# A hybrid layer's recurrences: the end of one block and the start of the next written step by step in turn

## The chip, the cores and the metric

The kernel runs on one core of a Trainium2 chip. The core has a matrix engine (TensorE, PE in the profile), a vector engine (VectorE, DVE), a scalar engine (ScalarE, ACT), a general engine (GpSimd, POOL) and a queue that issues transfers (SyncE, SP). Each works through its own queue in order and waits on semaphores for the others. The metric is the device time of one launch in microseconds; lower is better.

## The reference, cut to what matters

The input is one sequence of 2048 tokens with 1024 features; 16 learned tokens are put in front (T = 2064 tokens). One layer is computed in 32-bit floats:

```
p = rms_norm(h) @ w_in                     # 1024 -> 512 (LRU) + 1544 (attention) + 1024 (RWKV)
oa = rg_lru(...)                           # causal conv, gates, h_t = a_t h_{t-1} + b_t, times gelu
ob = forgetting_attention(q, k, v, f)      # 8 heads of 64, causal softmax with a decay term
oc = rwkv7(...)                            # 4 heads of 64, below
h = h + rms_norm(concat(oa, ob, oc) @ w_out)
f = causal_dwconv3(rms_norm(h) @ ffn_up)   # 1024 -> 2 x 2816
h = h + rms_norm((gelu(gate) * val) @ ffn_down)
```

The RWKV group is a recurrence over the tokens, with a state S of 64 x 64 for each head:

```
s_kk = S @ kk_t
S = S * w_t - outer(s_kk, kk_t * a_t) + outer(v_t, k_t)
o_t = S @ r_t
```

The decay w_t, the gate a_t and the vectors come from the projected features by small projections; after the recurrence follow a norm for each head, a bonus term and an output gate.

## The kernel before

**Stages.** First comes the input projection, in three parts of the sequence; beside it run the two recurrences (RWKV and RG-LRU). Then comes attention in two halves of the queries, with the output projection filled in; then the feed-forward part. Every large product is made of three matmuls on split operands (lines 174 to 176: high by high, low by high, high by low).

**The input projection.** In each part it goes through tiles of columns; one *unit* is one tile of 128 columns with one block of tokens, 24 matmuls into the tile `psp`. It writes its result to a scratch array in DRAM, `scr["p"]`, from which recurrence and attention load.

**The recurrence.** `Rwkv.block(b)` works on one block of 256 tokens (block 8: 64), in chunks of 64 tokens. It is a generator: each `yield` ends a step. It has two sections.
- The *opening* makes everything that doesn't need the state: mixing with the token before, the small projections (tile `eps`, lines 1049 to 1100), the products inside a chunk (L1124, tile `rps`), their transposes (L1153) and a triangular solve of 15 dependent turns, a product on POOL (L1171) and a sum on DVE (L1172) each. It ends with `yield self.SOLVED`.
- The *ending* has ten steps: the solve's small blocks are combined by 32 x 32 products (L1195 on PE, with DVE's L1205, L1212, L1219 and copies L1226, L1231 between them), then 64-wide products (L1247 and L1262, copied from PSUM by DVE's L1248 and L1263 and ACT's L1249 and L1264), L1274, the four turns of the state (L1282 on PE, L1286 on DVE), the outputs (L1313, L1318), the norm (L1323 to L1331), the gate (L1338, L1342) and the store (L1352) into `scr["mix"]`.

`lru_block` does the RG-LRU for the same tokens, in four steps (gates L1433, L1434; scan L1451; store L1461).

All PSUM tiles of the recurrence come from two pools: `rps` has two buffers, `eps` has one.

**How they are put beside each other.** `recurrences(..., part)` is a generator over the steps for three blocks. It is driven by `Beside` (PACE = 1.25 steps for each unit of the projection, from the fourteenth of part 0 on). What is left at the end of the projection is run by `beside.finish()`, and the very last ending, that of block 8, by the loop behind it; then the recurrence's memory is given back by `rec.close()`.

**What sets the order.** The program is written in that order, and a scheduler then builds each engine's queue: it takes the written order as a priority and lets instructions of other work pass where its plan has something late. So a change in the written order changes all queues, also beyond the lines that are edited.

**Attention's first tiles.** `Attn` takes the keys and queries from DRAM (k L527, q L553 and L554 on SP), and POOL clears and fills rows of the key tiles (L491, L492). Products: row maxima `mx` (L566), scores `sc` (L693, L694), outputs `po` (L716). The first two key tiles take room that the projection gives back after its last `psp`; the third, which the second half of attention begins with, takes room that `rec.close()` gives back.

Of the kernel before, what the change touches and what calls it, by code (L numbers as in the profile page):

```python
# [445 lines left out]
class Attn:  # L446
# [47 lines left out]
    def next(self, s):  # L494
        self.turn[s] = (self.turn[s] + 1) % len(self.ring[s])
        return self.ring[s][self.turn[s]]
# [908 lines left out]
def lru_block(core, R, scr, k, b):  # L1405

    nc = core.nc
    t0 = max(0, Rwkv.start(b))
    n = min(T, Rwkv.start(b + 1)) - t0
    c0 = PAD + t0  # L1410
    tt = nc.vector.tensor_tensor
    stt = nc.vector.scalar_tensor_tensor

    def tl(s):
        return R.t([P, 256], s, bufs=2 if s == "lu" else 1)[:, :n]

    def raw(row, a):
        t = R.t([P, 260], "lraw", bufs=2)[:, : c0 + n - a]
        nc.sync.dma_start(t, scr["p"][row : row + P, a : c0 + n])
        return t  # L1420

    for p in range(2):
        pc = slice(p, p + 1)
        x = raw(P * p, c0 - 3)
        u, r, g, al = (tl("l" + s) for s in ("u", "r", "g", "a"))
        nc.scalar.activation(u, x[:, 3:], AF.Identity, scale=k["conv_w"][:, 6 + p : 7 + p], bias=k["conv_b"][:, pc])
        for i in range(3):
            stt(u, x[:, i : n + i], k["conv_w"][:, 2 * i + p : 2 * i + p + 1], u, op0=ALU.mult, op1=ALU.add)


        ps = R.pe()
        pa, px = ps[:, :n], ps[:, 256 : 256 + n]
        nc.tensor.matmul(pa, k["ga_w"][:, p], u, start=True, stop=True)  # L1433
        nc.tensor.matmul(px, k["gx_w"][:, p], u, start=True, stop=True)  # L1434
        nc.scalar.activation(r, pa, AF.Abs, bias=k["ga_b"][:, pc])
        nc.vector.tensor_scalar(al, pa, k["ga_b"][:, pc], 0.0, op0=ALU.add, op1=ALU.min)
        nc.scalar.activation(g, px, AF.Tanh, scale=0.5, bias=k["rate"][:, 2, pc])
        nc.scalar.activation(r, r, AF.Tanh, scale=0.5)
        nc.scalar.activation(al, al, AF.Exp)
        stt(r, r, 1.0, al, op0=ALU.add, op1=ALU.mult)  # L1440
        stt(g, g, 1.0, u, op0=ALU.add, op1=ALU.mult)
        yield
        nc.scalar.activation(al, r, AF.Exp, scale=k["rate"][:, 0, pc])
        nc.scalar.activation(r, r, AF.Tanh, scale=k["rate"][:, 1, pc])

        tt(u, al, al, op=ALU.mult)
        stt(r, u, 1.0, r, op0=ALU.add, op1=ALU.mult)
        nc.vector.tensor_scalar(r, r, 1e-34, None, op0=ALU.max)
        nc.scalar.activation(r, r, AF.Sqrt)
        stt(g, g, 0.5, r, op0=ALU.mult, op1=ALU.mult)  # L1450
        nc.vector.tensor_tensor_scan(u, al, g, k["h"][:, pc], op0=ALU.mult, op1=ALU.add)  # L1451
        nc.vector.tensor_copy(k["h"][:, pc], u[:, n - 1 : n])

        ya, y = raw(2 * P + P * p, c0), r
        nc.scalar.activation(y, ya, AF.Square)
        nc.vector.tensor_scalar(y, y, 0.044715, 1.0, op0=ALU.mult, op1=ALU.add)
        tt(y, y, ya, op=ALU.mult)
        nc.scalar.activation(y, y, AF.Tanh, scale=0.7978845608028654)
        stt(y, y, 1.0, ya, op0=ALU.add, op1=ALU.mult)
        stt(u, u, 0.5, y, op0=ALU.mult, op1=ALU.mult)  # L1460
        nc.sync.dma_start(scr["mix"][P * p : P * p + P, t0 : t0 + n], u)  # L1461
        yield
# [600 lines left out]
def recurrences(core, R, lk, f_bias, scr, blocks, part):  # L2063


    for blk in blocks:
        gate_block(core, R, f_bias, scr, blk[2])
        yield
    for b in ((0, 1, 2), (3, 4, 5), (6, 7, 8))[part]:
        gen = R.block(b)  # L2070
        while next(gen) != R.SOLVED:
            yield
        yield from R.ending
        R.ending = gen
        yield from lru_block(core, R, scr, lk, b)


_INS = [
# [9 lines left out]
def hybrid_block_kernel(ctx: ExitStack, tc: tile.TileContext, args, out):  # L2088
# [25 lines left out]
    with ExitStack() as p1:  # L2114
# [7 lines left out]
        with ExitStack() as p1a:  # L2122
# [6 lines left out]
            for part in range(3):  # L2129
# [31 lines left out]
                for whole in units:  # L2161
                    if whole and i == READY + 1:
                        beside.add(recurrences(core, R, lk, a["fox_f_bias"], scr, blocks, part))
                    beside.advance()
                    if not whole:
                        continue
                    if part == 1 and i > 1:
                        next(split_out, None)
                    if part and i % 2 == 0:
                        with tc.issue_after(core.loaded.ins):  # L2170
                            next(sums, None)
                    i += 1
# [185 lines left out]
```

## Time and profile before

| | us |
|---|---|
| median of 3 runs | 3013.33 (3009.2 to 3013.38) |
| the profiled execution | 3015.7 |
| its span in the profile | 3014.0, mean clock of PE 0.969 |
| PE, 40 to 875 (projection) | 814.51 busy of 835 |
| PE, 875 to 1123 (first half of attention, rest of the recurrence) | 228.88 busy of 248, clock 0.85 |
| PE, 1123 to 1150 (step to the second half) | 23.97 busy of 27, clock 0.62 |
| PE, 1150 to 1540 | 381.63 busy of 390, clock 1.00 |
| PE, 1540 to 1600 | 47.69 busy of 60, clock 0.86 |
| PE, 1600 to 3014 (feed-forward) | 1388.66 busy of 1414, clock 1.00 |

The stretches are cut by the times at which the last `psp` product (874.96), the first use of the third key tile (1133.16) and the following stages show in the trace. "Busy" is the time in which PE had a matmul in it; the clock is the share of the full TensorE clock that was granted, so busy times clock is work at full speed. In a timeline a row is start, duration, engine, line, operation, written tile <- read tiles, shape, and in square brackets the idle time of the engine before it with what ended it. `x32` means a group of 32 instructions in a row.

### The profile page before, as it was taken

Reading aid. Unit: us, or ns where it says so; the run is one execution under the profiler, and the core shown is the slowest. Engines: PE = TensorE matmul, PEld = TensorE weight load, DVE = VectorE, ACT = ScalarE, POOL = GpSimd, SP = SyncE. Lnnn points to the kernel's source line nnn. Section 1 sums busy time; section 2 is a strip of 40 time slices with the busy share of each in tenths; the row PEclk is TensorE's granted clock in tenths of the full one; section 3 lists DMA queues with packets and bytes.
Section 4 is the critical chain, followed back from the end, with each engine's and each line's share of the span. In section 5 each row is a group of like instructions: output and inputs, shape, how many; then the busy total and the mean of one; then the engine's idle time right before and its main releaser. Section 6 shows DMA issues by size and latency. Waiting matters only on the chain.

```text
span 3014.0 us, 52809 instructions
## 1 busy us (share of the span) xinstructions
PE 2901.1 (96%) x18694; PEld 2488.9 (83%) x18694; DVE 2037.7 (68%) x3937; ACT 1480.0 (49%) x2858; POOL 1324.4 (44%) x1569
## 2 busy tenths in 40 slices
PE   6999999999999999999979999999999999999998
PEld 6998889888886655666558999999999999787887
DVE  5268645665676776556635898798778777656766
ACT  4246333443345554445634666666566665424333
POOL 1001121222223666666852467455645544656443
PEclk8999999999988899999989999999999999999999
DMA  6776569576653347545245565577677764436453
GB/s 216 235 243 209 169 228 319 173 231 202 201 134 82 95 110 214 121 115 121 59 139 165 166 203 179 170 210 217 206 213 217 215 200 129 161 114 220 143 177 119
DMA packets 469190, 530.49 MB, mean 176 GB/s; under 512 B 85710, under 2 KB 355736, under 8 KB 467372
## 3 DMA queue, kind: packets, MB, share of 16 engines
q1 hardware_dynamic: 468156, 526.17, 58.0%
q8 instruction: 147, 2.41, 0.3%
q0 software_dynamic: 768, 0.93, 0.1%
q14 instruction: 119, 0.97, 0.1%
HBM read 368.07 MB, written 158.90 MB: 175 GB/s over the span
## 4 chain that ended last, share of the span: by engine, by line
PE 59%; DVE 5%; POOL 2%; issue 2%; ACT 2%; DMA 1%; SPq 0%; DVEq 0%; POOLq 0%; ACTq 0%
PE psu L174 9%; PE psu L175 9%; PE psu L176 9%; PE po L716 4%; PE psd L174 4%; PE psd L175 4%; PE psd L176 4%; PE mx L566 2%; PE sc L693 2%; PE pswo L174 2%; PE pswo L176 2%; PE pswo L175 2%; PE sc L694 2%; DVE mc L571 1%; ACT p L698 0%
## 5 line engine op out<-in xcount | busy, mean ns | idle before, releaser
L174 PE MATMUL psu<-xo,uw 128*128 128x344 f32 x1848 | 587.9, 322 | 5.9 <-ACT ga L1821 3.3
L175 PE MATMUL psu<-xo,uw 128*128 128x344 f32 x1848 | 592.2, 321 | 0.0
L176 PE MATMUL psu<-xo,uw 128*128 128x344 f32 x1848 | 582.2, 320 | 0.0
L174 PE MATMUL psp<-xh,wh 128*128 128x384 f32 (+2 forms) x1152 | 379.6, 330 | 0.0
L176 PE MATMUL psp<-xh,wl 128*128 128x384 f32 (+2 forms) x1152 | 376.9, 327 | 0.0
L175 PE MATMUL psp<-xl,wh 128*128 128x384 f32 (+2 forms) x1152 | 376.5, 327 | 0.0
L1650 DVE TENSOR_TENSOR uw<-uq,uw 128x512 fp32r<-128x512 f32 x341 | 320.9, 946 | 59.5 <-ACT uw L1649 57.1
L174 PEld LDWEIGHTS psu<-xo,uw 128*128 128x128 f32 x1848 | 346.5, 188 | 7.5 <-ACT ga L1821 3.6
L175 PEld LDWEIGHTS psu<-xo,uw 128*128 128x128 f32 x1848 | 347.8, 188 | 0.0
L176 PEld LDWEIGHTS psu<-xo,uw 128*128 128x128 f32 x1848 | 346.3, 188 | 0.0
L1649 ACT ACTIVATE uw<-uq 128x512 fp32r<-128x512 f32 x462 | 287.7, 627 | 89.7 <-PE psu L176 41.6
L571 DVE TENSOR_REDUCE mc<-mx 128x1 f32<-128x512 f32 (+6 forms) x352 | 190.2, 565 | 117.8 <-PE mx L566 84.3
L698 ACT ACTIVATE p<-sc,bias 128x512 f32<-128x512 f32 (+4 forms) x352 | 197.5, 590 | 142.5 <-PE sc L694 120.5
L1789 DVE SCALAR_TENSOR_TENSOR uy<-psu,ffn_cols,uy 128x342 f32<-128x342 f32 (+1 forms) x390 | 220.5, 567 | 63.5 <-ACT uy L1787 62.5
L1650 POOL TENSOR_TENSOR uw<-uq,uw 128x512 fp32r<-128x512 f32 x121 | 180.6, 1492 | 157.7 <-ACT uw L1649 134.9
L1797 POOL TENSOR_TENSOR uy<-uy,uy 128x342 f32<-128x342 f32 (+1 forms) x132 | 145.8, 1105 | 228.0 <-DVE uy L1789 64.0
L737 POOL TENSOR_TENSOR acc<-acc,p 128x512 f32<-128x512 f32 (+3 forms) x208 | 223.3, 1075 | 45.9 <-DVE acc L737 21.7
L174 PEld LDWEIGHTS psp<-xh,wh 128*128 128x128 f32 x1152 | 219.2, 190 | 8.7 <-issue 7.3
L176 PEld LDWEIGHTS psp<-xh,wl 128*128 128x128 f32 x1152 | 219.1, 190 | 7.0 <-issue 5.1
L175 PEld LDWEIGHTS psp<-xl,wh 128*128 128x128 f32 x1152 | 219.1, 190 | 5.0 <-issue 3.2
L1650 DVE TENSOR_TENSOR fo<-u,fo 128x896 fp32r<-128x896 f32 x88 | 100.9, 1146 | 132.7 <-ACT fo L1649 132.2
L1649 ACT ACTIVATE fo<-u 128x896 fp32r<-128x896 f32 x88 | 81.2, 923 | 208.5 <-PE psd L176 112.6
(483 smaller groups left out, 6426.8 us busy)
## 6 DMA issues: line engine op xcount, KB each, us to landing
uq<-scr_us SPq DMA_DIRECT2D x220, 256.0 KB
uq<-in_ffn_up_dram SPq DMA_DIRECT2D x209, 256.0 KB
wl<-scr_wk SPq DMA_DIRECT2D x48, 512.0 KB
wh<-scr_wk SPq DMA_DIRECT2D x48, 512.0 KB
u<-scr_ff SPq DMA_DIRECT2D x88, 256.0 KB
scr_ff<-uy SPq DMA_DIRECT2D x110, 171.0 KB
raw<-in_w_in_dram SPq DMA_DIRECT2D x24, 512.0 KB
scr_wk<-wh SPq DMA_DIRECT2D x24, 512.0 KB
```

Source lines behind the costliest of these rows:

```text
L174: nc.tensor.matmul(out, ah, bh, start=first, stop=False, skip_group_check=more)
L175: nc.tensor.matmul(out, ah, bl, start=False, stop=False, skip_group_check=more)
L176: nc.tensor.matmul(out, al, bh, start=False, stop=last, skip_group_check=more)
L566: nc.tensor.matmul(ps[:rows, : e - a], q3[:, qo : qo + rows], k2[:, a:e], start=True, stop=not last)
L571: self.reduced = nc.vector.tensor_reduce(mc[:rows, i, ci : ci + 1], ps[:rows, : e - a], axis=AX.X, op=ALU.max)
L698: last = nc.scalar.activation(p[:rows, :w], ps[:rows, :w], AF.Exp, bias=bias[:rows, j : j + 1])
L716: mm = nc.tensor.matmul(po[at : at + 64, c0:n], v1[:rows, j], p[:rows, : n - c0], start=start and i < 2, stop=end and i + 2 >= len(group), ...
L737: eng.tensor_tensor(a, ps_[0][0][:rows, c0:n] if start and i == 1 else a, p[:rows, : n - c0], op=ALU.add)
L1649: core.nc.scalar.activation(hi, src, AF.Copy)
L1650: (eng or core.nc.vector).tensor_tensor(lo, src, hi, op=ALU.subtract)
L1789: core.conved = stt(y[:, :n], src[:, i : n + i], cw[:, 44 * i + cc : 44 * i + cc + 1], y[:, :n], op0=ALU.mult, op1=ALU.add)
L1797: core.pooled = nc.gpsimd.tensor_tensor(v[:, :n], g[:, :n], v[:, :n], op=ALU.mult)
```

## The change

In `recurrences` the steps of a block were written one section after another: the opening of block b, the whole ending of block b-1, the RG-LRU of block b. Now there are two chains: the ending of block b-1, and the opening of block b followed by its RG-LRU. One step of each is written in turn, and when one chain is done, the other goes on alone. The instructions are the same. The opening has one step more (a `yield` after the solve), so a block has 19 steps in place of 18 and the first one 9 in place of 8. The ending of block 8 is left over as before.

```diff
     for b in ((0, 1, 2), (3, 4, 5), (6, 7, 8))[part]:
         gen = R.block(b)
-        while next(gen) != R.SOLVED:
+
+        def opening():
+            while next(gen) != R.SOLVED:
+                yield
             yield
-        yield from R.ending
+            yield from lru_block(core, R, scr, lk, b)
+
+        chains = [R.ending, opening()]
+        while chains:
+            chain = chains.pop(0)
+            for _ in chain:
+                chains.append(chain)
+                yield
+                break
         R.ending = gen
-        yield from lru_block(core, R, scr, lk, b)
```

How the queues of the engines change shows at three places. On PE, inside the projection, the small products of the ending of block 1 (`rps` tiles are PSUM results, `rwxu` and `rwsc` tiles of the recurrence; `psp` is the projection). Before:

```order
L1195 MATMUL rps_3649<-rwxu_3562 32x32 x16
L1195 MATMUL rps_3667<-rwxu_3562 32x32 x32
L176 MATMUL psp_4339<-xh_3093,wl_4308 128x384
L174 MATMUL psp_4339<-xh_3093,wh_4307 128x384
L175 MATMUL psp_4339<-xl_3094,wh_4307 128x384
L176 MATMUL psp_4339<-xh_3093,wl_4308 128x384
L1195 MATMUL rps_3730<-rwxu_3562,rwsc_2159 32x32 x16
```

The changed kernel at the same products, with the projection's rows in the middle left out:

```order
L1195 MATMUL rps_3553<-rwxu_3315 32x32 x16
L1195 MATMUL rps_3571<-rwxu_3315 32x32 x32
L174 MATMUL psp_3876<-xh_3058,wh_3790 128x384
...
L1124 MATMUL rps_3636<-rwrav_3533,rwbk_3540 128x128 x4
...
L1124 MATMUL rps_3649<-rwrav_3533,rwbk_3540 128x128 x4
L1195 MATMUL rps_3698<-rwxu_3315,rwsc_2376 32x32 x16
```

Where four projection matmuls stood ahead of the last group there are now 37 and the next block's chunk products (L1124); in the other endings there are as many or more. Between later groups of the ending (L1247, L1262) there are 17 to 20 in most places. In all, the recurrence's instructions on PE stand in 382 separate pieces beside the projection and attention, before in 374.

On PE, at the end of the projection and the start of attention. Before:

```order
L175 MATMUL psp_10080<-xl_6567,wh_9817 128x256
L176 MATMUL psp_10080<-xh_6566,wl_9818 128x256
L1247 MATMUL rps_9191<-rww_973_7341,rwxf_8880 64x128 x4
L1262 MATMUL rps_9237<-rwsc_7340,rwxu_9169 64x128 x8
L1100 MATMUL eps_9753<-rwsq_9660,bones 128x512
L1262 MATMUL rps_9248<-rwsc_7340,rwxu_9169 64x128 x8
L1274 MATMUL rps_9260<-rww_973_7341,rwsc_7340 64x64 x16
L1282 MATMUL rps_9260<-rstate,rwgt_9235 64x64 x4
```

The changed kernel:

```order
L175 MATMUL psp_10010<-xl_6479,wh_9757 128x256
L1313 MATMUL rps_9530<-rstate,rwrav_7465 64x64 x8
L1318 MATMUL rps_9530<-rww_991_7567,rwsc_7566 64x64 x8
L176 MATMUL psp_10010<-xh_6478,wl_9758 128x256
L1100 MATMUL eps_9866<-rwsq_9733,bones 128x512
L693 MATMUL sc_11235<-q_1458_11146,k_1448_11109 128x512
```

The ending of block 5 now lies ahead of the last projection matmul, where it followed it before; one product of the recurrence (L1100) is left between that matmul and attention.

On PE, the end of the recurrence (L1342 is its last product) and the first use of attention's third key tile (`k_1963`). Before, the end of that stretch:

```order
L1342 MATMUL rps_11081<-rwsg_10414,g_up 128x64
L693 MATMUL sc_13122<-q_1922_12765,k_1453_11120 128x512
L694 MATMUL sc_13122<-q_1452_11118,k_1454_11121 128x512
...
L693 MATMUL sc_13277<-q_1974_12943,k_1448_11109 128x512
L693 MATMUL sc_13282<-q_1974_12943,k_1448_11109 128x512
L566 MATMUL mx_12950<-k_1963_12902,q_1456_11125 128x400
```

The changed kernel:

```order
L1342 MATMUL rps_11081<-rwsg_10421,g_up 128x64
L693 MATMUL sc_12831<-q_1852_12520,k_1453_11120 128x512
L694 MATMUL sc_12831<-q_1457_11129,k_1454_11121 128x512
...
L566 MATMUL mx_12873<-k_1454_11121,q_1451_11114 128x128
L568 LDWEIGHTS identb
L568 MATMUL mx_12873<-futureb,identb 128x128
L766 MATMUL mx_12855<-oh_12852,ones_col 1x512
L566 MATMUL mx_12953<-k_1963_12902,q_1456_11125 128x512
```

The last product of the recurrence moved forward by 53 rows of attention (from its 576th to its 523rd on PE), the first use of the tile by 40 (from the 596th to the 556th). Between the two lay 20 rows, of scores and outputs alone, and now lie 33, with row maxima among them. On SP the recurrence's last store (L1352) is followed by the load of that tile (L527) in both orders.

## The prediction

> **What bounds the kernel now.** I read the page first, for the engine that carries the end; then the stretches of TensorE by stage; then its waits inside the input projection; last the timelines of three places where it loses time. The page:
>
> ```profile
> span 3014.0 us, 52809 instructions
> PE 2901.1 (96%) x18694; PEld 2488.9 (83%) x18694; DVE 2037.7 (68%) x3937; ACT 1480.0 (49%) x2858; POOL 1324.4 (44%) x1569
> PEclk8999999999988899999989999999999999999999
> PE 59%; DVE 5%; POOL 2%; issue 2%; ACT 2%; DMA 1%; SPq 0%; DVEq 0%; POOLq 0%; ACTq 0%
> ```
>
> TensorE (PE) is the bound: 96% busy, and most of the chain that ends last. An edit that removes no matmul can only win idle time of PE, or time in which its granted clock was low. The dips of the clock lie in slices 1, 12 to 14 and 23. By stage, PE alone (columns: stretch, length, busy, clock, DMA share, GB/s):
>
> ```profile
> 45.00:875.00 830.00, 809.51 (x6783) 0.97 0.67 216
> 875.00:1123.00 248.00, 228.88 (x1977) 0.85 0.45 104
> 1123.00:1150.00 27.00, 23.97 (x78) 0.62 0.71 141
> 1150.00:1500.00 350.00, 345.91 (x1603) 1.00 0.49 126
> 1600.00:3014.00 1414.00, 1388.66 (x7794) 1.00 0.59 180
> ```
>
> The input projection runs to 875, the first half of attention with the rest of the recurrence to 1123, the step to the second half to 1150, the rest of attention to 1500. That rest, without the recurrence, is 99% busy at clock 1.00. Whatever the recurrence costs besides its own matmuls therefore lies before 1150, and this change moves only the recurrence. All that follows 1150 I leave as it is: its order on PE is nearly the same, at a cost of nothing as long as it starts in the same state.
>
> **The waits inside the projection.** The ending's small products are the longest wait there (us in total, times, longest), and the second wait of that list is a third of it:
>
> ```profile
> PE rps L1195 <- DVE rwxu L1212: 7.7, 4, 3.5
> PE rps L1195 <- ACT rwsc L1154: 2.5, 2, 1.7
> ```
>
> One of the four, on PE and then on DVE:
>
> ```profile
> 396.70 2.18 PE L1195 MATMUL rps<-rwxu 32*32 32x32 f32 x96
> 398.81 0.44 PE L176 MATMUL psp<-xh,wl 128*128 128x384 f32 x1
> 399.09 0.34 PE L174 MATMUL psp<-xh,wh 128*128 128x384 f32 x1
> 399.27 0.34 PE L175 MATMUL psp<-xl,wh 128*128 128x384 f32 x1
> 399.45 0.34 PE L176 MATMUL psp<-xh,wl 128*128 128x384 f32 x1
> 402.00 1.21 PE L1195 MATMUL rps<-rwxu,rwsc 32*32 32x32 f32 x32 [2.21 <-DVE rwxu L1212]
> 403.63 0.52 PE L175 MATMUL psp<-xl,wh 128*128 128x384 f32 x1
> 403.95 0.52 PE L176 MATMUL psp<-xh,wl 128*128 128x384 f32 x1
> ```
>
> ```profile
> 400.06 0.25 DVE L1172 TENSOR_REDUCE rwix<-rwitmp 128x8 f32<-128x112 f32 x1
> 401.28 0.67 DVE L1212 TENSOR_TENSOR rwxu<-rps,rwxu 32x512 f32<-32x512 f32 x1
> ```
>
> The products end at 398.88 (396.70 + 2.18); VectorE (DVE), whose queue holds steps of the next block's solve and of the LRU ahead of it, finishes the sum that they feed at 401.95: 3.1 us. The queue of PE has four projection matmuls for that time, 0.18 us apart (399.27 to 399.45), so PE stands 2.21 us. Afterwards the matmuls come 0.32 us apart (403.63 to 403.95): the clock is halved. Three stretches of 10 us (busy of PE, PEld, DVE, ACT, POOL; then clock) show that for three of the waits:
>
> ```profile
> 400.00:410.00 10.00, 8.00 (x81) 7.69 (x82) 5.25 (x14) 1.52 (x2) 1.02 (x2) 0.83 0.31 93
> 670.00:680.00 10.00, 10.00 (x109) 8.24 (x107) 8.85 (x21) 4.09 (x8) 3.07 (x5) 0.69 0.31 95
> 760.00:770.00 10.00, 8.38 (x112) 7.91 (x106) 7.24 (x19) 3.64 (x8) 4.12 (x7) 0.66 0.68 213
> ```
>
> Lost to the clock: 1.7 + 3.1 + 3.4 = 8.2 us. With the 7.7 of waiting, these four waits cost 15.9 us, 4.0 each.
>
> In the new order 37 projection matmuls stand between these products and the ones that need the sum, at 0.18 us 6.7 us against the 3.1 needed; for the other blocks it is as many or more. So the four waits should end. What is late next: the DVE steps of the solve, which lay among the early steps of the ending, now lie among its later copies (L1248, L1263). There the order gives 17 to 20 projection matmuls a step, 3.1 to 3.6 us, about the 3.1 that are needed. Ends: all won and nothing new, -16; one wait of 4.0 us in each of the six endings that the projection now carries, 24 - 16 = +8. I take **-8**, half of the win, since spacing and delay are so near.
>
> The Trainium skill ("TensorE: Matmul & The Clock Gate", Part 1) says that the clock gate goes to half after an idle window of about 3.4 us. By it a wait of 2 us costs only itself and this term would be at most -7.7; the rows above show the halving behind a wait of 2.21 us, so I go by them.
>
> **The bursts.** A burst of small products costs the next projection matmul: 0.28 us to its successor (398.81 to 399.09) against 0.18, plus about as much in front. The order cuts the recurrence into 382 pieces on PE in place of 374: 8 x 0.1 to 0.2, **+1**.
>
> **The part boundaries.** At the first boundary:
>
> ```profile
> 280.00:310.00 30.00, 23.68 (x301) 18.47 (x299) 27.66 (x77) 24.00 (x46) 10.69 (x19) 0.67 0.41 138
> ```
>
> DVE is 92% busy and PE has 30 - 23.68 x 0.67 = 14.1 us less than its full work. There the new order has a little less DVE work, at the second boundary more, with three groups of the recurrence in it. I take **+1**, with a third of the 14.1 to either side as ends (-5 and +5).
>
> **The start of attention.** PE, with one group at full clock for comparison; then the queue of SP, POOL, and the stretches:
>
> ```profile
> 327.46 1.20 PE L1274 MATMUL rps<-rww,rwsc 128*64 128x64 f32 x32
> 874.96 0.41 PE L176 MATMUL psp<-xh,wl 128*128 128x256 f32 x1
> 882.81 2.03 PE L1274 MATMUL rps<-rww,rwsc 128*64 128x64 f32 x32
> 887.52 0.46 PE L566 MATMUL mx<-k,q 128*128 128x144 f32 x1
> ```
>
> ```profile
> 880.45 0.45 SPq L553 DMA_DIRECT2D q<-scr_qh  x1
> ```
>
> ```profile
> 883.58 3.60 POOL L492 MEMSET k<- 1x2080 f32 x2
> ```
>
> ```profile
> 880.00:890.00 10.00, 8.84 (x85) 6.48 (x84) 8.36 (x21) 0.00 (x0) 5.71 (x4) 0.50 0.53 119
> 890.00:900.00 10.00, 9.51 (x88) 7.13 (x84) 8.13 (x22) 2.82 (x6) 0.00 (x0) 0.50 1.02 216
> ```
>
> Between the last projection matmul (875.37) and the first of attention (887.52) PE works only for the recurrence: 12.15 us at half clock, worth 7.1 at full (x 1.20 / 2.03), so 5.0 are lost; and 887.5 to 900 at 0.50 loses 6.2: 11.3 in all. The new order puts that work ahead of the last projection matmul, where it costs its 7.1 us, and leaves PE one product before attention. The cover is then gone: attention waits for its own loads and for POOL, which clears and fills two key tiles, two pairs of memsets of 3.60 us each. POOL no longer has a memset of the recurrence in front, so PE should stand about 7.2 us. How long the clock stays halved after that no row tells: not at all gives 7.2 - 11.3 = -4; as long as now, with an empty stretch as long as the present one, 12.15 + 6.2 - 11.3 = +7. I take **-2**: a short empty stretch, and half clock for a few microseconds.
>
> **The step to the second half of attention.** PE, SP, POOL:
>
> ```profile
> 1120.77 0.36 PE L1338 MATMUL rps<-ident,rwxu 64*128 64x64 f32 x1 [3.14 <-DVE rwxu L1331]
> 1122.94 0.69 PE L1342 MATMUL rps<-rwsg,g_up 128*128 128x64 f32 x2
> 1133.16 1.07 PE L566 MATMUL mx<-k,q 128*128 128x400 f32 x3 [0.59 <-POOL k L492]
> ```
>
> ```profile
> 1124.06 0.39 SPq L1352 DMA_DIRECT2D scr_mix<-rwxu  x1
> 1124.54 0.45 SPq L527 DMA_DIRECT2D k<-scr_kh  x1
> ```
>
> ```profile
> 1131.29 1.82 POOL L492 MEMSET k<- 1x2080 f32 x1
> ```
>
> The third key tile takes the recurrence's room. Its chain is: the last products (end 1123.63), the last store, then the load behind it on SP, then POOL's fill, ended at 1133.11, and the first product on the tile: 9.5 us, in which PE has some twenty short matmuls. In 1123 to 1150 PE does 23.97 x 0.62 = 14.9 us of full-clock work, a loss of 12.1; with the wait of 3.14 ahead it is 15.3.
>
> In the new order the recurrence's last product stands 53 rows earlier against attention, and 32 matmuls lie between it and the first use of the tile, scores, row maxima and outputs mixed. At 345.91 / 1603 = 0.216 us each that is 6.9 us against 9.5: 2.6 us of waiting stay, and I allow as much again for the clock. That leaves 5 of 15.3, taken as **-11**. Ends: -15 when nothing remains; 0 when the store still comes as late.
>
> **The sum.** -8 + 1 + 1 - 2 - 11 = -19, from the profiled execution's 3015.7 (span 3014.0): 2996.7. That execution lies 2.4 above the median of 3013.3, so the forecast is **2994**. What a measurement here can tell from no change is 0.2%, 6 us.
>
> **The rivals.**
> *Slower: the waits move to the copies.* Opening and ending now share two PSUM banks and one DVE queue all along. Against a step's 3.1 to 3.6 us stands a delay of 3.1; if the solve's steps hold L1248's or L1263's copies some 0.5 us longer, PE stands at both steps of all six endings, and the row above says that 2 us of standing halve the clock: 12 x 4.0 = 48 against 16 won, +32 where I have -8: **3034**. For it: DVE is the busiest of PE's partners; against: in the old order other steps have passed at that spacing without a wait in the list.
> *Moved evenly.* One such wait an ending, +8 for -8: **3010**, within 0.2%.
> *Attention starts empty.* The empty stretch is as long as the present one and the clock stays halved as now: +7 for -2, **3003**. The gate rule of the Trainium skill's page speaks for this one: an empty stretch of 7 us is two of its windows, and the first matmuls would run at half. The trace has no empty stretch of that length inside the projection to show it.
> *The step does not clear.* The recurrence ends no earlier, since its own chain and not PE's order sets its end: 0 for -11, **3005**. For it: PE's wait of 3.14 for L1331 is a wait for that chain; against: 53 rows of lead.
>
> **How the numbers follow.** The forecast 0.43 (its own range 2982 to 3003), copies 0.21, moved evenly 0.15, empty start 0.12, step not cleared 0.09. Faster by over 0.2% (below 3007): 0.43 + 0.12 + 0.09 less a little where two of them meet, 0.61. Same: 0.15 and that little, 0.17. Slower: 0.22. For 8 in 10 the range takes most of the last case's road, up to 3029, and down to 2976, where about all of the waits and of the step are won.
>
> **What would show it.** Right: no wait of L1195 for L1212 of over 1 us and clocks above 0.9 where now 0.66 to 0.83 stands; the first product of attention at most 8 us behind the last of the projection; the last store of the recurrence at least 8 us earlier against attention, and the 27 us behind it at a clock near 0.9. Wrong: PE waits for DVE's L1248, L1263 or L1286 of several microseconds in sum with half clock behind them; a projection that ends later than its added work (7 to 11 us of recurrence) explains.

## The result and the profile after

The changed kernel takes 3020.0 us (median of 19 runs, 3010.8 to 3027.4), the kernel before, run beside it, 3009.4 (19 runs, 3003.3 to 3017.4). The ratio is 1.0027 (95% interval 1.0019 to 1.0036): 8 us slower by the ratio (the medians lie 10.6 apart), where the forecast was 19 us faster. The time lies inside the range that was given, but on the other side of no change: the range reached that far only to hold the slower rivals. Single executions of either kernel scatter by some 15 us; the profiled one of the changed kernel took 3018.4, and a second trace of each kernel was taken below, so that a stage's difference can be told from scatter.

The page of the changed kernel has the same shape as before, with a little less busy time of PE and a longer span:

```profile
span 3016.7 us, 52807 instructions
PE 2895.9 (96%) x18694; PEld 2494.4 (83%) x18694; DVE 2039.6 (68%) x3937; ACT 1481.6 (49%) x2858; POOL 1308.6 (43%) x1569
PEclk8999899999988899999989999999999999999999
```

To see where the time went, both traces are cut at the same places of the work: the last projection matmul, the first matmul of attention, its 520th and 750th row in PE's queue, the first matmul of the feed-forward part, the end. PE alone (stretch, length, busy, clock, DMA share, GB/s), the kernel before:

```profile
40.00:875.40 835.40, 814.91 (x6812) 0.97 0.67 215
875.40:887.50 12.10, 10.94 (x94) 0.50 0.55 128
887.50:1081.60 194.10, 180.62 (x1608) 0.85 0.42 97
1081.60:1150.20 68.60, 61.08 (x355) 0.83 0.62 135
1150.20:1662.40 512.20, 491.52 (x2249) 0.98 0.48 131
1662.40:3014.00 1351.60, 1326.26 (x7513) 1.00 0.59 182
```

The changed kernel:

```profile
40.00:882.20 842.20, 832.28 (x6982) 0.97 0.66 213
882.20:894.00 11.80, 0.88 (x3) 0.64 0.72 165
894.00:1088.80 194.80, 177.13 (x1608) 0.85 0.41 96
1088.80:1145.70 56.90, 49.09 (x277) 0.94 0.56 129
1145.70:1664.50 518.80, 492.46 (x2247) 0.97 0.48 133
1664.50:3016.90 1352.40, 1327.31 (x7513) 0.99 0.59 182
```

The second traces, at the rows that matter. Of the kernel before (projection, gap, attention's first rows, 750th row to feed-forward):

```profile
40.00:877.50 837.50, 820.73 (x6814) 0.97 0.66 214
877.50:889.60 12.10, 10.94 (x95) 0.50 0.55 128
889.60:1079.50 189.90, 178.47 (x1608) 0.86 0.42 99
1148.10:1661.70 513.60, 491.65 (x2248) 0.98 0.48 131
```

Of the changed kernel:

```profile
40.00:883.80 843.80, 832.01 (x6973) 0.97 0.66 212
883.80:895.30 11.50, 0.80 (x3) 0.61 0.71 170
895.30:1089.80 194.50, 176.13 (x1608) 0.86 0.40 97
1146.50:1665.80 519.30, 492.43 (x2248) 0.97 0.48 132
```

Length less busy time is PE's idle time. Mean of the two traces of each kernel, in us:

| stage | length before | after | idle before | after |
|---|---|---|---|---|
| projection | 836.5 | 843.0 | 18.6 | 10.9 |
| gap ahead of attention | 12.1 | 11.7 | 1.2 | 10.8 |
| attention to its 520th row | 192.0 | 194.7 | 12.5 | 18.0 |
| 520th to 750th row | 68.6 | 56.8 | 7.5 | 7.6 |
| 750th row to the feed-forward part | 512.9 | 519.1 | 21.3 | 26.6 |
| feed-forward part | 1351.2 | 1352.3 | 25.4 | 24.7 |
| sum | 2973.2 | 2977.5 | 86.5 | 98.5 |

PE's idle time grew by 12 us. Half-clock time, summed from the clock records of the traces, is 167 and 171 us before and 162 and 165 after. A low clock costs nothing while PE stands; counted only while PE was busy, it is 143 and 148 us before and 132 and 134 after, so some 6 of the 12 us came back there.

The stages are 4.3 us longer in sum, not 8: both traced executions of the kernel before lay above its median (3015.7 and 3013.9 against 3009.4), those of the changed kernel near its own. So the table places about half of the loss, and where the rest lies these traces don't show. What it does show is this: up to the 750th row, where both kernels have done the same work, the changed kernel is 3.0 us ahead (1106.2 against 1109.2); behind that row, with the same matmuls, it loses 7.3.

**The projection** won what was forecast. The wait of L1195 for L1212, 7.7 and 7.1 us in the two traces of before, is gone; the list now begins with two others (us in total, times, longest):

```profile
PE rps L1195 <- issue: 3.8, 2, 2.9
PE psp L174 <- DMA wh<-scr_wk: 2.0, 1, 2.0
```

The stage is nevertheless 6.5 us longer, with some 165 more matmuls of the recurrence in it.

**The gap** kept its length and lost its content. PE, then DVE, SP and POOL:

```profile
881.85 1.02 PE L1100 MATMUL eps<-rwsq,bones 128*128 128x512 f32 x2
893.79 1.10 PE L693 MATMUL sc<-q,k 128*128 128x512 f32 x2 [10.92 <-DMA q<-scr_qh]
```

```profile
884.07 0.42 DVE L241 SCALAR_TENSOR_TENSOR stl<-psp,sth 128x256 fp32r<-128x256 f32 x1
893.07 1.56 DVE L489 MEMSET q<- 1x512 f32 x3 [0.16 <-DVE rwgsm L1328]
```

```profile
884.64 0.42 SPq L243 DMA_DIRECT2D scr_ql<-stl  x1
885.15 0.47 SPq L527 DMA_DIRECT2D k<-scr_kh  x1
888.86 0.60 SPq L555 DMA_DIRECT2D q<-scr_qh  x1
```

```profile
883.85 3.62 POOL L492 MEMSET k<- 1x2080 f32 x2
```

PE does not wait for POOL, which is done at 887.47, but for two other things that end together. One is the loads: the projection's last result has to leave PSUM (L241, behind steps of the recurrence on DVE), go to DRAM and come back, and SP issues the loads of k and q one after the other from 885.15. The last that this product needs, that of L555, landed at 893.59 by the semaphore records of the trace. The other is DVE, which clears and fills rows of the q tiles between steps of the recurrence; the weight load (PEld) of the same product waits for the first of the three fills of L489, done at 893.56:

```profile
PEld sc L693 <- DVE q L489: 11.7, 1, 11.7
```

In the second trace the load landed at 894.89 and the fill ended at 895.02. The kernel before has the same fills:

```profile
886.93 1.03 DVE L489 MEMSET q<- 1x512 f32 x2 [0.16 <-DVE rstate L1286]
```

The first of these two ended at 887.42, and attention's first product followed at 887.52, 12.1 us behind the projection's last. So attention's inputs take as long as before; only now PE has nothing to do meanwhile. No run shows by how much the gap would shrink if the loads alone or the fills alone came sooner.

**The step to the second half of attention** cleared almost as forecast:

```profile
1115.79 0.33 PE L1342 MATMUL rps<-rwsg,g_up 128*128 128x64 f32 x2
1125.44 0.50 PE L566 MATMUL mx<-k,q 128*128 128x512 f32 x1 [1.68 <-POOL k L492]
```

From the end of the recurrence's last product (1116.12) to the first product on the tile it is 9.3 us, before 9.5, now filled with attention's products but for 1.7 us; and the clock between the 520th and the 750th row rose from 0.83 to 0.94. **Behind it**, where nothing was to change, two new stalls stand, the first at 1152.5. PE, ACT, POOL:

```profile
1152.54 0.80 PE L693 MATMUL sc<-q,k 128*128 128x512 f32 x1 [2.56 <-ACT p L698]
1219.63 0.18 PE L693 MATMUL sc<-q,k 128*16 128x16 f32 x1 [2.37 <-ACT p L698]
```

```profile
1151.80 1.26 ACT L698 ACTIVATE p<-sc,bias 128x512 f32<-128x512 f32 x2 [6.73 <-POOL acc L737]
1217.59 1.06 ACT L168 ACTIVATE mh<-raw 128x1024 fp32r<-128x1024 f32 x1 [4.22 <-DMA raw<-scr_mix]
```

```profile
1150.51 1.26 POOL L737 TENSOR_TENSOR acc<-p,p 128x512 f32<-128x512 f32 x1 [4.03 <-DMA scr_den<-acc]
```

In the first, POOL may not write a sum over the old one before that one's store has landed; ACT waits for POOL, PE for ACT. In the second, ACT stands 4.2 us before a row of the output projection whose input isn't there, and attention's L698 stands behind it in the same queue. PE stands 2.4 to 2.6 us in each, and the clock is low after each (0.66 for 1150 to 1160, 0.83 for 1218 to 1228):

```profile
1150.00:1160.00 10.00, 7.46 (x33) 4.33 (x33) 3.03 (x8) 4.82 (x9) 8.98 (x8) 0.66 0.52 116
1218.00:1228.00 10.00, 8.37 (x35) 3.83 (x35) 5.43 (x15) 5.47 (x12) 5.66 (x11) 0.83 0.37 90
```

### The profile page after: what moved, and what is told of

The parts are those of the page before. It is cut to its first block, busy times and chain, and to the rows that moved or that the text cites. A ratio compares the mean times of both kernels' runs of the same rounds, so it can differ in the third digit from the quotient of the medians.

```text
span 3016.7 us, 52807 instructions
## 1 busy us (share of the span) xinstructions
PE 2895.9 (96%) x18694; PEld 2494.4 (83%) x18694; DVE 2039.6 (68%) x3937; ACT 1481.6 (49%) x2858; POOL 1308.6 (43%) x1569
## 4 chain that ended last, share of the span: by engine, by line
PE 80%; DVE 6%; DMA 5%; POOL 3%; ACT 3%; issue 2%; SPq 0%; DVEq 0%; POOLq 0%; ACTq 0%
PE psu L174 9%; PE psu L175 9%; PE psu L176 9%; PE psp L176 6%; PE psp L174 6%; PE psp L175 6%; PE psd L174 4%; PE psd L175 4%; PE psd L176 4%; PE po L716 3%; PE pswo L174 2%; PE sc L693 2%; PE pswo L175 2%; PE pswo L176 2%; PE mx L566 2%
## 5 line engine op out<-in xcount | busy, mean ns | idle before, releaser
L698 ACT ACTIVATE p<-sc,bias 128x512 f32<-128x512 f32 (+4 forms) x352 | 197.4, 591 | 182.2 <-PE sc L694 153.3
L571 DVE TENSOR_REDUCE mc<-mx 128x1 f32<-128x512 f32 (+6 forms) x352 | 190.6, 565 | 113.6 <-PE mx L566 87.0
```

The source lines that it names most:

```text
L571: self.reduced = nc.vector.tensor_reduce(mc[:rows, i, ci : ci + 1], ps[:rows, : e - a], axis=AX.X, op=ALU.max)
L698: last = nc.scalar.activation(p[:rows, :w], ps[:rows, :w], AF.Exp, bias=bias[:rows, j : j + 1])
```

## The experiments

All ratios are to the kernel before, run on the same chip beside them. Blocks "one after the other" are written as in the kernel before, the others step by step in turn.

### The changed kernel again; less pace; the turns in one half

Theory "cover": the loss comes from recurrence work pushed out of the gap into a busy projection. Rival "weave": the turns cost by themselves. First the changed kernel as it is:

> The changed kernel once more, for a second trace beside the first. Both theories: ratio to the kernel before 1.002 to 1.0036; PE stands 10 to 12 us between the projection's last product and attention's first (10.9 in the first trace), waits of L1195 for L1212 below 1 us in sum. What differs from the first trace by several microseconds is scatter of a single execution and carries no argument.

Measured: 1.0028 (1.0017 to 1.0039). Its trace is the second one above: 10.7 us empty, and no wait of L1195 for L1212 in the list of PE's waits in front (L1124 waits for it once, 1.1 us).

```diff
-PACE = 1.25
+PACE = 1.1
```

> The changed kernel with PACE 1.1 in place of 1.25: the recurrence is written later against the projection, 44 of its products lie between the projection's last product and attention's first (before: 47, changed kernel: 1), and its last product keeps the same place as in the changed kernel (523rd row of attention). Theory 'cover' (the change loses because recurrence work that stood in the gap ahead of attention and in its first half was pushed into the projection, where PE was busy anyway): PE's empty 10.9 us at the start fall to 1 to 2 us, ratio to the kernel before 0.9990 to 1.0005, that is 7 to 11 us under the changed kernel. Rival 'weave' (steps of two blocks in turn on DVE and in two PSUM banks cost by themselves, above all in attention's first half): no more than 3 us under the changed kernel, ratio 1.0017 to 1.003.

Measured: 1.0026 (1.0011 to 1.0042). The gap is filled again (10.40 us, busy 6.16 at clock 1.00), and nothing is won:

```profile
866.60:877.00 10.40, 6.16 (x89) 1.00 0.77 186
877.00:1077.70 200.70, 178.26 (x1614) 0.86 0.40 94
```

The idle time went into attention's rows to the 520th, 22.4 us in place of 18.0. The traced execution took 3009.3, 10 us under the median of its kernel, so its stages can't show the whole loss. "Cover" falls as an account of the loss all the same: the gap is covered and the ratio is that of the changed kernel.

```diff
         chains = [R.ending, opening()]
+        if b not in (6, 7, 8):
+            while next(gen) != R.SOLVED:
+                yield
+            yield from R.ending
+            R.ending = gen
+            yield from lru_block(core, R, scr, lk, b)
+            continue
```

(The added lines make the blocks that aren't in the tuple run one after the other; in the next diffs of this kind only the line with the tuple is shown.)

> Only blocks 6 to 8 are written in turn (part 2 of the sequence), blocks 0 to 5 as in the kernel before. 44 products of the recurrence lie in the gap ahead of attention, the last one stands at attention's 523rd row. The waits of L1195 for L1212 in the projection's first two parts stay (6 to 8 us in sum). Theory 'cover': the gap is covered and the step to the second half of attention is won (11 to 17 us), ratio 0.9950 to 0.9975. Rival 'weave': attention's first half, where steps of two blocks alternate, still loses the 10 to 14 us that the changed kernel's trace shows there, ratio 0.999 to 1.001.

Measured: 1.0040 (1.0026 to 1.0054), by the median more than the whole change, though the intervals overlap.

```diff
+        if b not in (0, 1, 2, 3, 4, 5):
```

> Only blocks 0 to 5 are written in turn, blocks 6 to 8 as in the kernel before. 33 products lie in the gap ahead of attention, the last product of the recurrence stands at the 547th row (before 576, changed 523). Theory 'cover': the waits for L1212 go (10 us of idle PE less before the projection's end), the gap is mostly covered (3 to 5 us empty), a part of the step to the second half is won: ratio 0.9955 to 0.998. Rival 'weave', with its price in the projection (bursts) as large as the waits that go: ratio 0.999 to 1.001, the projection no shorter than before once its added recurrence work is taken off.

Measured: 1.0007 (0.9993 to 1.0021). In its projection PE is idle 10.6 us, so the win of the waits is there without the rest; 8.2 us of the gap are empty, and none of the win is seen at the end. Neither theory gives both this and the run before it.

### How much of the recurrence is left, and which blocks

Theory "filler": attention's first part waits on its own chains and needs the recurrence's products to fill it. Rival "order": the queues of the kernel before fit, and any other order gives idle time back.

```diff
-PACE = 1.25
+PACE = 1.0
```

> The changed kernel with PACE 1.0: 1548 of the recurrence's 2304 products lie ahead of the projection's last product (kernel before 1636, changed kernel 1720), 76 in the gap ahead of attention. Theory 'filler' (attention's first half waits on its own chains and needs recurrence products to fill it; the changed kernel has too few left): PE's idle time from the end of the projection to attention's 750th row falls from 36 to 22 us or less, the projection keeps its 9 to 10 us less idle time, ratio to the kernel before 0.996 to 0.9985. Rival 'order' (what fills attention is not the amount but that the queues of the kernel before happen to fit there; any other order of the recurrence's rest gives idle time back): idle 30 us or more in that stretch and 8 or more from the 750th row to the 1500th (before 3), ratio 1.0005 to 1.003.

Measured: 1.0053 (1.0034 to 1.0072). With more filler left than before, PE's idle time from the projection's end to the 750th row is 43.6 us. "Filler" falls.

```diff
+        if b not in (8,):
```

> Only block 8 is written in turn with the ending of block 7; every queue of PE is that of the kernel before up to attention's first half (first different row 4283 of 14131), the recurrence's last product moves from attention's 576th row to its 570th. Theory 'filler': same amount of filler, idle time from the end of the projection to the 750th row 18 to 25 us (before 22), ratio 0.997 to 1.0005. Rival 'order': 28 us or more there and 8 or more between the 750th and the 1500th row, ratio 1.001 to 1.004.

Measured: 1.0001 (0.9988 to 1.0013).

```diff
+        if b not in (7, 8):
```

> Blocks 7 and 8 in turn with the endings of 6 and 7; PE's queue is that of the kernel before up to row 4045, just behind attention's start. Same expectations as for block 8 alone: 'filler' 18 to 25 us idle to the 750th row and ratio 0.997 to 1.0005; 'order' 28 us or more and ratio 1.001 to 1.004.

Measured: 0.9994 (0.9979 to 1.0008); idle to the 750th row 23.0 us, and 61.4 us from the 520th to the 750th row with clock 0.92 in place of 68.6 with 0.83. Most of these 7 us are only moved: the rows to the 520th take 198.3 us in place of 192.0, with 43 more matmuls in them. Up to the 750th row some 2 us are won, too few to show in the whole.

The kernel before, not the changed one, with

```diff
-PACE = 1.25
+PACE = 1.4
```

> The kernel before, nothing written in turn, with PACE 1.4 in place of 1.25: as many recurrence products ahead of the projection's last product as before (1636) and in the gap (47), the last one at the 570th row, but other orders from row 1564 on. Theory 'filler': no difference, ratio 0.999 to 1.001, idle to the 750th row 18 to 25 us. Rival 'order': 28 us or more there, ratio 1.001 to 1.004, with no weaving at all.

Measured: 1.0054 (1.0034 to 1.0073), with no turns at all. Its idle time is that of before (86.6 us); the mean clock of its runs is 0.967 (before 0.971), and its trace has 69 us of half clock in the projection (before 42 and 53), which at half speed is some 10 of the 16 us lost. "Order" stands, though what a new order costs here is clock and not idle time.

### The recurrence's place against attention

Theory "lead": the turns win in the projection and lose because the recurrence then runs ahead of attention. Rival "order" as above. Blocks 0 to 5 in turn, and the recurrence held at the end of the projection:

```diff
+        if b not in (0, 1, 2, 3, 4, 5):
...
+                    held = 0
...
-                    beside.advance()
+                    held += part == 2
+                    if held <= 38:
+                        beside.advance()
```

> Blocks 0 to 5 written in turn, 6 to 8 one after the other, and no step of the recurrence advanced beside the last units of the projection's part 2 (after 38 of its yields): the recurrence's place against attention is that of the kernel before (46 products in the gap, before 47; last one at the 572nd row, before 576). Theory 'lead' (the turns win 7 to 10 us of PE idle time in the projection, and all is lost because the recurrence then runs ahead: an empty gap, and a second half of attention that begins early and stalls between the 750th and the 1500th row): idle 9 to 12 us in the projection, 1 to 4 in the gap, 3 to 5 from the 750th to the 1500th row, ratio 0.9965 to 0.9985. Rival 'order' (whatever is won in one stretch comes back in another, wherever the recurrence stands): total idle time of PE 88 us or more, as before, ratio 0.9995 to 1.003.

Measured: 1.0036 (1.0023 to 1.0049). The place is that of before and the projection's win is there (8.9 us idle), and the kernel is slower:

```profile
40.00:861.80 821.80, 812.90 (x6798) 0.98 0.68 218
861.80:873.10 11.30, 6.16 (x93) 0.92 0.67 150
1071.60:1141.20 69.60, 59.96 (x352) 0.88 0.57 124
1141.20:1660.50 519.30, 494.45 (x2248) 0.97 0.48 131
```

"Lead" falls. (The profiled execution took 3013.9, 6 under the median of its kernel; its stages can't account for the whole.)

```diff
+        if b not in (0, 1, 2):
...
-PACE = 1.25
+PACE = 1.2
```

> Only blocks 0 to 2 written in turn, PACE 1.2: 47 products in the gap, the last one at the 570th row. Theory 'lead': a win of the projection's first two parts alone, 3 to 6 us less idle time there, all else as before: ratio 0.9975 to 0.9995. Rival 'order': 0.9995 to 1.003.

Measured: 1.0024 (1.0015 to 1.0033). This changes the pace too; the pace of 1.2 without turns is measured below.

```diff
+        if b not in (6,):
```

> Only block 6 written in turn with the ending of block 5 (the pair that lies at the projection's end). Blocks 7 and 8 in turn cost nothing, 6 to 8 cost 0.4%, so block 6 is the difference. Its last product is at the 570th row, as with 7 and 8 alone. Theory 'lead': what costs is not block 6 in turn but that the recurrence ends at the 523rd row; so idle from the 750th to the 1500th row 3 to 5 us, gap 4 to 6, ratio 0.9995 to 1.0015. Rival 'order' (turns at the projection's end cost by themselves): ratio 1.003 to 1.005, as for blocks 6 to 8.

Measured: 1.0039 (1.0026 to 1.0052). The recurrence ends at the 570th row, as with 7 and 8, and the loss is that of 6 to 8. So among the pairs it is this one, at the projection's end, that loses by itself; blocks 0 to 5, and 7 and 8, lose little or nothing. The losses don't add, since the changed kernel has this pair too and loses less. Its trace has 29.3 us of idle time from the 750th row to the feed-forward part (before 21.3). The stalls behind the 750th row stand here too (2.8 and 3.0 us), so the recurrence's lead isn't what makes them.

```diff
+        if b not in (0, 1, 2, 3, 4, 5, 6, 7):
```

> The changed kernel, but block 8 written one after the other: everything to the gap is the changed kernel's (1720 products ahead, 1 in the gap), the last product moves from the 523rd row back to the 547th. Theory 'lead': the gap stays empty (10 to 11 us), and idle from the 750th to the 1500th row falls from 8.6 to 4 to 7: ratio 1.0005 to 1.0025. Rival 'order': as the changed kernel, 1.002 to 1.004.

Measured: 1.0034 (1.0022 to 1.0046): the changed kernel's loss without its last pair of turns.

### Other orders without turns

What was left open is whether the turns have a price of their own. The kernel before with two more paces:

```diff
-PACE = 1.25
+PACE = 1.2
```

> The kernel before with PACE 1.2, nothing in turn; orders differ from row 1255 of 14131, 47 products in the gap, last one at the 550th row. Theory 'any new order costs': ratio 1.002 to 1.005. Rival 'the turns cost': ratio 0.999 to 1.001.

Measured: 1.0020 (1.0008 to 1.0031). The same pace with blocks 0 to 2 in turn, above, has 1.0024: these turns cost nothing that can be told.

```diff
-PACE = 1.25
+PACE = 1.3
```

> The kernel before with PACE 1.3, nothing in turn; orders differ from row 1574, 47 products in the gap, last one at the 570th row. Theory 'any new order costs': ratio 1.002 to 1.005. Rival 'the turns cost': ratio 0.999 to 1.001.

Measured: 1.0035 (1.0023 to 1.0048). Both lose, as theory "any new order costs" has it. In the first of them the stall of the changed kernel stands again, for the same store (PE, then POOL):

```profile
1147.98 0.79 PE L693 MATMUL sc<-q,k 128*128 128x512 f32 x1 [4.45 <-ACT p L698]
```

```profile
1145.94 1.26 POOL L737 TENSOR_TENSOR acc<-p,p 128x512 f32<-128x512 f32 x1 [4.70 <-DMA scr_den<-acc]
```

And its gap is half empty (10.90 us, busy 4.79), though as many recurrence products stand in it as before.

Second traces:

> The kernel before itself, for a second trace. If the idle times by stage repeat: 18 to 22 us in the projection, 1 to 2 in the gap, 12 to 15 in attention's rows to the 520th, 7 to 9 to the 750th, 3 to 4 to the 1500th, in all 86 to 92, and clock losses that differ from the first trace by up to 25 us of half clock. Ratio 0.999 to 1.001.

Measured: 1.0009 (1.0000 to 1.0018), which shows how small a ratio can be read here: the kernel before against itself gives 0.09%. Idle time 84.2 us in all: 16.8 in the projection, 1.2, 11.4, 7.6, 4.5 in the stretches after it (before 20.5, 1.2, 13.5, 7.5, 3.2).

> Blocks 0 to 5 in turn once more, for a second trace. If idle time repeats and the clock scatters: 9 to 12 us idle in the projection, 7 to 9 in the gap, 16 to 18 to the 520th row, 6 to 8 between the 750th and the 1500th, in all 92 to 97; half clock well above the first trace's 128 us, since that execution lay 7 us under the median of its kernel. Ratio 0.9995 to 1.002.

Measured: 1.0017 (1.0002 to 1.0033). Idle time 92.5 us (first trace 94.6), half clock 161 us (first 128): idle time repeats within a few microseconds, the clock scatters by tens.

## Why the prediction was wrong

The forecast named two right wins and took the rest of the kernel for unmoved. Up to the 750th row its sum promised 19 us and the traces show 3.0; behind it, it put the cost at nothing and the traces show 7.3. Three steps failed: the start of attention, attention's first part, and all that follows 1150, which turned the sign. Term by term, each with the mean of two traces:

- **The waits in the projection, -8.** The number is right, in part by luck. The four waits are gone, and PE's idle time is 7.8 us less (7 to 10 less with blocks 0 to 5 alone). But the term priced them at 16 with the half clock behind them and took half of that for fear of new waits. The new waits at the later copies, the rival at 3034, did not come: L1263 and L1286 aren't among the waits of over half a microsecond. The clock did not come back either: half clock behind those waits is gone, but other pauses have it now (in the first trace 1.95 us ahead of 477.98 and 2.87 ahead of 722.81), and the projection's half-clock time is 46 us after and 48 before.
- **The bursts, +1, and the part boundaries, +1.** Too small to be seen.
- **The start of attention, -2.** Mis-sized, and ascribed to the wrong wait. I priced POOL's memsets, 7.2 us, and put the loads and DVE's fills of q at nothing more, though the row of those fills stood in the trace of before. POOL was done 5.5 us behind the projection's last product, the loads and fills 11.6 us behind it. By the sum's own reckoning, 11.7 us are empty, and the 12.5 us behind, at clock 0.66 and 0.67, lose 4.2; less the 11.3 of before that is +4.6. The rival of an empty start, +7, had the right mechanism; the clock came back sooner than it assumed. Here the Trainium skill's rule ("TensorE: Matmul & The Clock Gate", Part 1), that an empty window halves the clock, agrees with the gap, where the clock is 0.64 and 0.61; its figure of about 3.4 us does not agree with the stalls behind the step, where 2.4 to 2.6 us were enough.
- **The step to the second half, -11.** Right in its mechanism, somewhat too large. The chain took 9.3 us where 9.5 were read, attention's products filled 7.6 of it where 6.9 were counted, and 1.7 us of waiting stayed where 2.6 were allowed. The 520th to the 750th row takes 11.8 us less, of which the clock is about 8 (17 us less half clock, 16 of them while PE was busy); the rest is 78 matmuls fewer, which stand elsewhere now and win nothing.
- **"All that follows 1150 I leave as it is", 0.** Wrong, and the step that turned the sign: from the 750th row to the feed-forward part PE is idle 5.3 us more, with 12 us more half clock, part of it within the idle time, in all 6.2 us of length with the same matmuls (2247 to 2249); the feed-forward part adds 1.1. The two stalls shown above are 4.9 us of it in the first trace and 4.6 in the second. The order on PE was nearly the same there, but that of SP, POOL and ACT, which I had not compared, was not.
- **Attention's first part**, for which the sum had no term: 5.5 us more idle time with the same 1608 matmuls. The longest waits up to the 750th row are attention's own (L566 for DVE's L571: 9.0 and 7.5 us, before 3.4 and 3.1); L1247 of the recurrence waits 2.4 and 2.8 us for ACT's L1249 besides, and did not before. No run settled which of the moved steps makes them.

What the runs show in place of a price for the turns: of the kernels tried, every one whose order differs from the kernel before inside the projection is slower by its median, by 0.07 to 0.54%, with turns or without them (blocks 0 to 5, the least, with 0.07 and 0.17, can't be told from the 0.09 of the kernel before against itself); the two that first differ in attention's first half (blocks 8; 7 and 8) are not slower. Three paces around 1.25 without turns lose 0.20, 0.35 and 0.54%. So the changed kernel's 0.27% needs no price of the turns, and the order of the kernel before is a good one among its neighbours. Whether the turns have a small price besides is open, and so is why an order costs clock in one kernel and idle time in another, and why block 6 in turn costs more than the rest. None of the kernels tried beats the kernel before by more than the measurement can tell.

## What to carry to other kernels

Where a scheduler builds all queues from the written order, an edit has two effects: the one that it is made for, which the trace of before can price, and a new draw of everything behind it, which the trace can't; in this kernel, whose order is a good one already, the second was a loss of some tenths of a per cent, so a forecast needs a term for it. It can be sized cheaply with kernels that change nothing but the order (here a pace of 1.2 or 1.3). And work that fills a wait is worth its time where it stands: ahead of attention 12 us passed with 94 matmuls in them and with 3. Putting it back by another pace brought no time back, since that was again a new order.

## What was not expected of the hardware

A pause of 2.4 to 2.6 us of PE can be followed by lowered clock (0.66 and 0.83 above), but its length alone does not decide it. With blocks 0 to 5 in turn, a pause of 2.42 us is followed by 10 us at full clock:

```profile
1139.80 0.50 PE L693 MATMUL sc<-q,k 128*128 128x512 f32 x1 [2.42 <-ACT p L698]
```

```profile
1139.80:1149.80 10.00, 10.00 (x59) 1.00 0.43 94
```

And one wait in the feed-forward part, 3.27 us in both traces of the kernel before, is followed by 10 us at 0.84 in one (from 1669.57) and at 1.00 in the other (from 1668.67).

The scatter of single executions, some 15 us, goes with the granted clock: over all runs here, each taken against the mean of its kernel, 0.001 of mean clock goes with 1.3 us, and two traces of one kernel (blocks 0 to 5) differ by 33 us in half clock (128 and 161) while their idle times differ by 2.
